# Gated MLP of an encoder block: the down-projection sums two row tiles in PSUM, convolution and gate keep their running value there, and the up products share three banks

## The chip, the core and the metric

The kernel is one program on one core of a Trainium2 chip. TensorE (PE in the profile; PEld is its weight load) multiplies into PSUM, which has eight banks of 512 float32 columns; VectorE (DVE) and ScalarE (ACT) read and write PSUM and SBUF; GpSimd (POOL) works on SBUF alone; SyncE (SP) issues the DMAs. The metric is device time in microseconds (us) of one launch. Lower is better.

## What is computed

One layer on x of 2048 tokens by 1024 channels, all float32: a mixer (attention and pooling), then the channel sub-layer, to which the change is confined:

```python
h2 = rmsnorm(x, norm2_g) * (1.0 + sc2) + sh2
u  = h2 @ w_up                                   # 1024 -> 2 * 2816
u  = u[t-1]*conv_w[0] + u[t]*conv_w[1] + u[t+1]*conv_w[2] + conv_b   # per channel
gate, val = u[..., :2816], u[..., 2816:]
out = x + g2 * ((silu(gate) * val) @ w_down)
```

## The kernel before

Every float32 matrix operand is split into a high and a low part, and a product is three matmuls (high by high, high by low, low by high) added in PSUM.

**Tiling of the MLP.** `PARTS` cuts the tokens into three parts of 640, 768 and 640 (5, 6 and 5 row tiles of 128); each part goes through 22 steps j, one for each 128 gate channels and their 128 value channels. The loop `for idx, (p, j) in enumerate(seq)` runs 66 steps. A step does four things side by side:

- `gen_up(p, j)`: the up-projection of one gate and one value tile, as seven products of a Strassen-Winograd scheme (`PROD`), 12 matmuls each (4 of k, 3 for the split), on 322 columns (386 in the middle part). Each product has a PSUM bank of its own (tag `pp`, five of them in rotation); `add` evicts product by product, one copy on ACT and seven additions on DVE, into `ug` and `uv` in SBUF. With `kmajor` (first step of the second and third part) all seven products run side by side over k.
- `gen_gate(p, j-1)`: convolution, silu, product and split of the step before: two `Identity` on ACT, four `scalar_tensor_tensor` on DVE, `Silu` on ACT, a multiplication on DVE, a copy to `gh` on ACT and a subtraction to `gl` on DVE. The running values `ac0` and `ac1` are SBUF tiles of 640 (768) columns.
- `gen_down(p, (j-2,), n)`: `down` multiplies the gate tile j-2 with the two 512-column halves of w_down, three matmuls into a `py` bank (three in rotation) for each row tile and half, and DVE adds the bank to the running sum `ys`. Without a pair: each sum takes one row tile of w_down.
- `gen_w(p, j+1)`: the seven weight operands of the next step: POOL forms the four sums, ACT copies each operand to its high part, POOL subtracts to the low part; seven buffers of each (`whi`, `wlo`). `gen_wd` does w_down: in the first part load, multiplication by the gate `g2` and subtraction on DVE, copy on ACT, and a store to DRAM; in later parts two loads.

**Order.** The generators are advanced by hand-written counts of up matmuls (`n % 11`, `n % 8`, `WS`); a planner then orders each engine's queue by data and free buffers, with the written order as priority, except instructions held by `keep_in_program_order`. On the chip each engine takes its queue in order. Between two parts `gen_ops` prepares seven moving operands for the next part, 4 k-slices each, on ACT, POOL and DVE, beside the last downs of the part; at the very end the last three row tiles are summed in `pl` banks and stored.

Of the kernel before, what the change touches and what calls it, by code (L numbers as in the profile page):

```python
# [18 lines left out]
P = 128  # L19
# [28 lines left out]
class InOrder:  # L48
    """An engine whose instructions stay in the order in which they are written."""
# [15 lines left out]
def hybrid_block(ctx: ExitStack, tc: tile.TileContext, x, c, w_ada, b_ada, norm1_g, w_in,  # L65
# [58 lines left out]
    # =============== mixer input projection ===============  # L124
    with tc.tile_pool(name="p1", bufs=1) as p1, \
            tc.tile_pool(name="ps1", bufs=1, space=PSUM) as ps1:
        # columns of w_in: q, k, v first (their space is free first), then u
# [173 lines left out]
        # scale and shift of the first norm; the first tokens' norm beside them  # L301
# [18 lines left out]
        # weights, split, in the order of use  # L320
# [19 lines left out]
        # 1/count at the clipped edges  # L340
# [108 lines left out]
        def gen_tr(tok, qhl, khl):  # L449
            """q as (hi, lo), k as (hi, hi) and (lo, one), transposed"""  # L450
# [25 lines left out]
        def windows(b, us, res):  # L476
            """column i is token t0 - 8 + i, at column 8 + i of u; the last block has 8 more"""
# [74 lines left out]
        def gen_early_max():  # L552
            """the row maxima of the first unit over the keys of the blocks that are done"""
# [75 lines left out]
    # =============== attention and output projection ===============  # L629
    ctx3 = ctx.enter_context(ExitStack())  # L630
    with tc.tile_pool(name="po", bufs=1, side="right", reuse_waits="tile") as po, \
# [8 lines left out]
        # per key tile: [v_lo 0 | v_hi 0 | ones | v_hi 1 | v_lo 1]  # L640
# [185 lines left out]
        def gen_out(c_, half, wait=0):  # L826
            """x1 = x + pool half, then x1 += attention half."""
# [17 lines left out]
        def gen_ln2(t, x1, junk, hts, bank, stat, wait):  # L845
            """normalised x1, transposed"""
# [31 lines left out]
        # the last chunk's output projection: the pool half first, in banks that the attention leaves  # L878
# [67 lines left out]
        # =============== gated conv MLP: Winograd's form of Strassen's product ===============  # L946
# [12 lines left out]
        def gen_ops(p, res):  # L959
            """the moving operands of part p, split"""  # L960
# [10 lines left out]
            for k in range(4):  # L971
# [35 lines left out]
                G.tensor_tensor(out=t2, in0=t2, in1=b21, op=ALU.subtract)  # L1007
# [7 lines left out]
        def gen_w(p, j, res):  # L1015
            """the stationary operands of one pair of column tiles, split, in the order of use"""
# [12 lines left out]
            def split(nm, src):  # L1029
                h_ = pv.tile([P, 4, P], F32R, tag="whi", name=f"wh_{nm}{p}_{j}", bufs=7)  # L1030
                l_ = pv.tile([P, 4, P], F32R, tag="wlo", name=f"wl_{nm}{p}_{j}", bufs=7)
# [7 lines left out]
            yield  # L1039
            s1, s2 = raw2(f"s1_{p}_{j}"), raw2(f"s2_{p}_{j}")  # L1040
# [3 lines left out]
            yield  # L1044
            split("a12", a12)
# [54 lines left out]
    with tc.tile_pool(name="p3", bufs=1, reuse_waits="tile") as p3, \  # L1100
# [5 lines left out]
        def gen_wd(p, j, n, tag=""):  # L1106
            """w_down times the gate, split: worked out with the first part, kept in DRAM for the others"""
# [9 lines left out]
            h_ = pool.tile(shape, F32R, tag=tag + "hi" if tag else "wdh", name=f"wdh{p}_{j}_{n}", bufs=7 if tag else 3)  # L1117
            l_ = pool.tile(shape, F32R, tag=tag + "lo" if tag else "wdl", name=f"wdl{p}_{j}_{n}", bufs=7 if tag else 3)
# [7 lines left out]
            else:  # L1126
# [7 lines left out]
        PROD = (("1", "a11", "b11"), ("6", "s2", "t2"), ("2", "a12", "b21"), ("7", "s3", "t3"),  # L1134
                ("5", "s1", "t1"), ("4", "a22", "t4"), ("3", "s4", "b22"))

        def gen_up(p, j, kmajor, res):
            o0, no, N = PARTS[p]
            w = wres.pop((p, j))
            o = ops[p]  # L1140
            ug = p3.tile([P, 772], F32, tag="ug", name=f"ug{p}_{j}", bufs=1)
            uv = p3.tile([P, 772], F32, tag="uv", name=f"uv{p}_{j}", bufs=1)
            p1s = p3.tile([P, 386], F32, tag="p1s", name=f"p1s{p}_{j}", bufs=1)[:, 0:N]
            w1 = p3.tile([P, 386], F32, tag="w1", name=f"w1{p}_{j}", bufs=1)[:, 0:N]
# [3 lines left out]
            def bank(i):  # L1148
                py = kmajor and i < 2
                return ps3_.tile([P, 512], F32, tag="py" if py else "pp", name=f"pp{PROD[i][0]}{p}_{j}",  # L1150
                                bufs=3 if py else 5)[:, 0:N]

            def prod(ps, i, k):
                (ah, al), (bh, bl) = w[PROD[i][1]], o[PROD[i][2]]
                for m, (l_, r_) in enumerate(((ah, bh), (ah, bl), (al, bh))):
                    mm = PE.matmul(ps, l_[:, k], r_[:, k, 0:N], start=k == 0 and m == 0, stop=k == 3 and m == 2)  # L1156
# [4 lines left out]
            def add(i, ps):  # L1161
                if i == 0:
                    S.copy(out=p1s, in_=ps)
                elif i == 1:
                    V.tensor_tensor(out=w1, in0=ps, in1=p1s, op=ALU.add)
                elif i == 2:
                    V.tensor_tensor(out=ug[:, 0:N], in0=ps, in1=p1s, op=ALU.add)
                elif i == 3:
                    V.tensor_tensor(out=w7, in0=ps, in1=w1, op=ALU.add)
                elif i == 4:  # L1170
                    V.tensor_tensor(out=uv[:, N:2 * N], in0=ps, in1=w7, op=ALU.add)  # L1171
                    V.tensor_tensor(out=w1, in0=ps, in1=w1, op=ALU.add)
# [101 lines left out]
        for idx, (p, j) in enumerate(seq):  # L1274
# [19 lines left out]
            for _ in gen_up(p, j, j == 0 and p > 0, res):  # L1294
# [3 lines left out]
                if n % 8 == 4:  # L1298
                    step(gate)
# [111 lines left out]
```

## Time and profile before

| | us |
|---|---|
| median of 3 runs (2737.05 to 2743.99) | 2742.21 |
| span of the profiled execution, first to last instruction | 2741.8 |
| MLP, first step to the end | 1458.5 |

The time of the profiled execution as a whole is not told apart from its span; the span lies within the three runs. Busy shares over the span: PE 95%, DVE 86%, POOL 64%, ACT 54%. The shares are means over stages with different limits: the attention fills the first half, and within the MLP the three parts differ. The page's 40 slices, the busy time by stretches, and groups of instructions within one stretch are read below.

### The profile page before, as it was taken

To read this page: it belongs to the slowest core of one execution; us is meant where nothing else is said; L and a number is where in the kernel's file an instruction comes from. 1 tells how busy PE (TensorE), PEld (TensorE's weight loads), DVE (VectorE), ACT (ScalarE), POOL (GpSimd) and SP (SyncE) were. 2 spreads that over 40 slices of the span, in tenths; PEclk is the share of its full clock that TensorE was granted. 3 is DMA by queue.
4 is the path that set the end of the run, shared out by engine and by line. 5 is a ranking of instruction groups with operands and counts; after the bars stand their busy time and mean duration, and the time that the engine had idled before them with its cause. 6 is when DMAs were issued, how large, how long until landed. Compare 5 with 4: busy or idle time off the path is not lost.

```text
span 2741.8 us, 39488 instructions
## 1 busy us (share of the span) xinstructions
PE 2594.1 (95%) x13439; PEld 2242.1 (82%) x13439; DVE 2370.5 (86%) x3526; ACT 1475.5 (54%) x2656; POOL 1767.0 (64%) x1397
## 2 busy tenths in 40 slices
PE   5899989999999999999899999899999998999999
PEld 5788867777776767767888888789999997999998
DVE  7778688989999998887999999978888888898886
ACT  5566457777778777775533443543333334533342
POOL 1222146556657666565888888697777776988883
PEclk9899989999999999999999999999999999999999
DMA  9685374331221222225444444443333224433332
GB/s 291 232 258 179 99 239 149 106 95 60 64 80 55 71 72 76 80 64 179 151 130 133 128 130 123 145 132 105 100 104 100 93 87 132 147 123 120 106 110 93
DMA packets 318164, 338.65 MB, mean 124 GB/s; under 512 B 24655, under 2 KB 226329, under 8 KB 317961
## 3 DMA queue, kind: packets, MB, share of 16 engines
q1 hardware_dynamic: 316953, 332.31, 38.4%
q0 software_dynamic: 1008, 3.81, 0.5%
q8 instruction: 106, 1.74, 0.3%
q14 instruction: 97, 0.79, 0.1%
HBM read 249.42 MB, written 86.63 MB: 123 GB/s over the span
## 4 chain that ended last, share of the span: by engine, by line
PE 36%; DVE 13%; issue 3%; ACT 1%; POOL 1%; POOLq 0%; DVEq 0%; ACTq 0%
PE pp L1156 23%; PE py L1233 13%; DVE y L1238 3%; DVE ac L1202 2%; DVE ac L1205 2%; DVE b L993 1%; DVE t L993 1%; ACT ac L1199 1%; PE pl L1354 1%; DVE wds L56 0%; DVE wdl L1123 0%; DVE ac L1212 0%; DVE ug L1176 0%; DVE uv L1171 0%; DVE uv L1174 0%
## 5 line engine op out<-in xcount | busy, mean ns | idle before, releaser
L1035 POOL TENSOR_TENSOR wl_s<-s,wh_s 128x512 fp32r<-128x512 f32 x260 | 390.3, 1502 | 187.8 <-ACT wh_s L1033 186.6
L1238 DVE TENSOR_TENSOR y<-py,y 128x512 f32<-128x512 f32 x620 | 418.5, 682 | 95.5 <-PE py L1233 94.8
L741 POOL TENSOR_TENSOR acc<-acc,ph 128x512 f32<-128x512 f32 x352 | 463.4, 1316 | 41.0 <-ACT ph L735 15.7
L1156 PE MATMUL pp<-t,wh_s 128*128 128x322 f32 (+1 forms) x1584 | 390.2, 322 | 7.0 <-DVE x L1072 3.2
L737 DVE TENSOR_TENSOR pl<-S,ph 128x512 fp32r<-128x512 f32 x512 | 348.7, 684 | 38.5 <-ACT S L736 31.5
L735 ACT ACTIVATE ph<-S 128x512 fp32r<-128x512 f32 x512 | 307.3, 600 | 131.9 <-PE S L732 116.2
L694 DVE TENSOR_REDUCE mx<-pmx 128x1 f32<-128x512 f32 x500 | 338.1, 681 | 27.0 <-PE pmx L692 25.2
L1035 POOL TENSOR_TENSOR wl_a<-wr,wh_a 128x512 fp32r<-128x512 f32 x195 | 312.9, 1605 | 22.7 <-ACT wh_a L1033 22.6
L1233 PE MATMUL py<-wdh,gh 128*128 128x512 f32 x674 | 275.7, 409 | 47.1 <-DVE y L1238 40.6
L736 ACT ACTIVATE S<-S 128x512 f32<-128x512 f32 x512 | 306.4, 598 | 0.0
L1156 PEld LDWEIGHTS pp<-t,wh_s 128*128 128x128 f32 x1584 | 282.2, 190 | 27.8 <-DVE t L993 4.1
L1033 ACT CAST wh_s<-s 128x512 fp32r<-128x512 f32 x264 | 161.9, 617 | 226.8 <-PE pp L1156 197.0
L1156 PE MATMUL pp<-b,wh_a 128*128 128x322 f32 (+1 forms) x1056 | 267.9, 323 | 1.3 <-DVE b L993 0.8
L1233 PE MATMUL py<-wdh,gl 128*128 128x512 f32 x674 | 268.8, 399 | 0.0
L1233 PE MATMUL py<-wdl,gh 128*128 128x512 f32 x674 | 268.8, 399 | 0.0
L1156 PE MATMUL pp<-t,wl_s 128*128 128x322 f32 (+1 forms) x792 | 254.3, 321 | 0.0
L724 PE MATMUL B<-pl,vt 128*128 128x512 f32 x512 | 210.5, 411 | 6.2 <-DVE pl L737 6.0
L1033 ACT CAST wh_a<-wr 128x512 fp32r<-128x512 f32 x198 | 122.3, 618 | 165.6 <-PE pp L1156 158.4
L723 PE MATMUL A<-ph,vt 128*128 128x512 f32 x512 | 204.7, 408 | 5.2 <-ACT ph L735 5.2
L692 PE MATMUL pmx<-kA,qa 128*128 128x512 f32 x500 | 203.3, 408 | 3.9 <-DMA kA<-k_scr 3.0
L739 POOL TENSOR_TENSOR acc<-ph,ph 128x512 f32<-128x512 f32 x32 | 41.3, 1290 | 256.8 <-ACT ph L735 226.9
L732 PE MATMUL S<-qb,kB 65*128 65x512 f32 x512 | 202.8, 402 | 1.1 <-ACT qb L702 0.8
(273 smaller groups left out, 6784.4 us busy)
## 6 DMA issues: line engine op xcount, KB each, us to landing
wr<-in_w_up_dram SPq DMA_DIRECT2D x132, 512.0 KB
wdh<-wd_scr SPq DMA_DIRECT2D x88, 256.0 KB
wdl<-wd_scr SPq DMA_DIRECT2D x88, 256.0 KB
stage<-in_w_ada_dram SPq DMA_DIRECT2D x36, 512.0 KB
x_scr<-x SPq DMA_DIRECT2D x48, 256.0 KB
wds<-in_w_down_dram SPq DMA_DIRECT2D x44, 256.0 KB
wd_scr<-wdh SPq DMA_DIRECT2D x44, 256.0 KB
wd_scr<-wdl SPq DMA_DIRECT2D x44, 256.0 KB
```

Source lines behind the costliest of these rows:

```text
L694: V.tensor_reduce(out=mx[:, qt, j:j + 1], in_=ps, axis=AX.X, op=ALU.max)
L723: PE.matmul(A, vt[:, kt, 192 * a:192 * a + P], ph, start=kt == 0, stop=kt == NKT - 1)
L724: PE.matmul(B, vt[:, kt, 64 + 64 * a:192 + 64 * a], pl, start=kt == 0, stop=False)
L735: S.activation(out=ph, in_=s, func=AF.Exp, scale=0.125)
L736: S.activation(out=s, in_=s, func=AF.Exp, scale=0.125)
L737: V.tensor_tensor(out=pl, in0=s, in1=ph.bitcast(F32), op=ALU.subtract)
L741: G.tensor_tensor(out=acc, in0=acc, in1=ph.bitcast(F32), op=ALU.add)
L1033: S.copy(out=hf, in_=src)
L1035: eng.tensor_tensor(out=lf, in0=src, in1=hf.bitcast(F32), op=ALU.subtract)
L1156: mm = PE.matmul(ps, l_[:, k], r_[:, k, 0:N], start=k == 0 and m == 0, stop=k == 3 and m == 2)
L1233: PE.matmul(ps, l_[:, ts_], r_, start=i == 0, stop=i == 3 * len(js) - 1)
L1238: V.tensor_tensor(out=ys[t][:, ns], in0=ps, in1=ys[t][:, ns], op=ALU.add)
```

## The change

- **Down-projection**: from step 3 on every second step runs downs, for the pair (j-3, j-2): six matmuls into one `py` bank, then one addition by DVE. Even steps have none. The last two steps of a part have none; the pair (L-3, L-2) goes into the change of parts (L is 21). The four w_down tiles of a pair have four buffers instead of three, and their work is spread as before, two a step.
- **Gate**: one PSUM tile `ac` of two banks holds the running value, first of the gate half, then of the value half; `Silu` writes an SBUF tile `ag`. `ug`, `uv`, `ag`, `gh`, `gl` share eight SBUF tiles (`utile`); before there was one `ug` and one `uv`.
- **Up products**: banks `px`, `pz`, `pw`, one of each. Products 1, 6, 5 are added up in `px` and 7, 4 in `pw` by the matmuls themselves; ACT copies the partial sums out between them (four copies instead of one), DVE adds four times instead of seven. The operand order becomes a11, a12, s2, s3, s1, a22, s4, and t4 has its sign turned. `whi` and `wlo` have six buffers instead of seven, that is fewer by one weight operand ahead.
- Counts of the interleaving change (`n % 7` for the gate, `76` for the downs, `WS`); the last halves go in another order. Removed comments do nothing.

```diff
             def split(nm, src):
-                h_ = pv.tile([P, 4, P], F32R, tag="whi", name=f"wh_{nm}{p}_{j}", bufs=7)
+                h_ = pv.tile([P, 4, P], F32R, tag="whi", name=f"wh_{nm}{p}_{j}", bufs=6)
...
+        def utile(nm, dtype=F32):
+            return p3.tile([P, 772], dtype, tag="u", name=nm, bufs=8)
...
-            ug = p3.tile([P, 772], F32, tag="ug", name=f"ug{p}_{j}", bufs=1)
-            uv = p3.tile([P, 772], F32, tag="uv", name=f"uv{p}_{j}", bufs=1)
+            ug, uv = (utile(f"{nm}{p}_{j}") for nm in ("ug", "uv"))
...
-                for i in range(7):
-                    ps = bank(i)
-                    for k in range(4):
-                        yield from prod(ps, i, k)
-                    add(i, ps)
+            X, Y, W = bank("px"), bank("pz"), bank("pw")
+            yield from run(X, "1")
+            S.copy(out=p1s, in_=X)
+            yield from run(Y, "2")
+            add(c11, Y, p1s)
+            yield from run(X, "6", False)
+            S.copy(out=u2s, in_=X)
+            yield from run(W, "7")
+            S.copy(out=w7, in_=W)
+            yield from run(X, "5", False)
+            add(c22, X, w7)
+            u3s = p3.tile([P, 386], F32, tag="p1s", name=f"u3s{p}_{j}", bufs=1)[:, 0:N]
+            S.copy(out=u3s, in_=X)
+            yield from run(W, "4", False)
+            add(c21, W, u2s)
+            Y = bank("pz")
+            yield from run(Y, "3")
+            add(c12, Y, u3s)
+        def ac_tile(nm):
+            return ps3_.tile([P, 1024], F32, tag="ac", name=nm, bufs=1)
...
-                t_ = p3.tile([P, 768], F32, tag=f"ac{gv}", name=f"ac{gv}{p}_{j}", bufs=1)[:, 0:no]
+                t_ = ac_tile(f"ac{gv}{p}_{j}")[:, 0:no]
...
                 if gv == 0:
-                    S.activation(out=t_, in_=t_, func=AF.Silu)
+                    ag = utile(f"ag{p}_{j}")[:, 0:no]
+                    S.activation(out=ag, in_=t_, func=AF.Silu)
...
-            V.tensor_tensor(out=ag, in0=ag, in1=av, op=ALU.mult)
+            V.tensor_tensor(out=t_, in0=t_, in1=ag, op=ALU.mult)
...
-            dn = chain2(gen_down(p, (j - 2,), 0, add), gen_down(p, (j - 2,), 1, add)) if 2 <= j < L else iter(())
+            dn = iter(())
+            if j % 2 and 3 <= j < L:
+                add = [residual(p, i) for i in (j - 3, j - 2) if p > 0 and i < 2 * nt]
+                dn = chain2(gen_down(p, (j - 3, j - 2), 0, add), gen_down(p, (j - 3, j - 2), 1, add))
+            wdg = chain2(*(ahead if p == 0 else wd_of(p, j)))
...
-                if (n - 4) * 2 * nt >= done * 78:
+                if (n - 6) * 2 * nt >= done * 76:
                     step(dn)
...
                 for n in range(2):
-                    dn = gen_down(p, (L - 2,), n)
+                    dn = gen_down(p, (L - 3, L - 2), n)
                     while step(dn):
-                        step(gate, G1)
-                        step(opg, O1 if n else O0)
+                        step(gate, 2)
+                        step(opg, n)
```

## Rows read from the trace of the kernel before

**Rows 1.** Busy time by stretches of the MLP; the first line names the columns.

```profile
core 0: us, PE busy (x) PEld busy (x) DVE busy (x) ACT busy (x) POOL busy (x), PEclk, DMA share, GB/s
1283.30:1367.80 84.50, 76.27 (x442) 71.56 (x443) 70.58 (x78) 43.56 (x75) 71.55 (x49) 0.92 0.54 170
1367.80:1478.40 110.60, 99.59 (x568) 89.73 (x567) 109.03 (x139) 42.66 (x71) 95.99 (x58) 1.00 0.44 136
1478.40:1731.10 252.70, 238.93 (x1373) 217.31 (x1373) 247.99 (x326) 102.54 (x170) 206.64 (x133) 1.00 0.41 125
1731.10:1842.00 110.90, 96.38 (x455) 83.48 (x454) 88.90 (x111) 58.87 (x101) 86.78 (x61) 0.92 0.44 142
1842.00:2257.30 415.30, 415.30 (x2157) 387.62 (x2156) 345.96 (x460) 152.13 (x218) 296.25 (x201) 1.00 0.31 98
2257.30:2360.00 102.70, 92.48 (x487) 82.06 (x486) 81.89 (x108) 53.15 (x95) 77.27 (x63) 0.95 0.44 143
2360.00:2706.30 346.30, 346.30 (x2042) 323.09 (x2041) 309.75 (x423) 139.04 (x216) 298.13 (x200) 1.00 0.35 111
```

**Rows 2.** Timeline of ACT in the first part: start, us, what.

```profile
1583.70 0.42 ACT L1163 COPY p1s<-pp 128x322 f32<-128x322 f32 x1
...
1604.75 0.42 ACT L1163 COPY p1s<-pp 128x322 f32<-128x322 f32 x1
```

**Rows 3.** Chain of work that ended last: start, us, what, how many.

```profile
1859.88 2.12 PE pp L1156 x12
1883.03 2.12 PE pp L1156 x12
...
2374.06 1.92 PE pp L1156 x13
2393.42 1.92 PE pp L1156 x13
```

**Rows 4.** The same chain inside one step of the third part.

```profile
2391.55 1.18 PE pp L1156 x8
2392.72 0.70 PE py L1233 x3
```

**Rows 5.** Groups in twelve steps of part one: busy us, mean ns | idle before.

```profile
L1238 DVE TENSOR_TENSOR y<-py,y 128x512 f32<-128x512 f32 x120 | 80.4, 678 | 0.0
...
L56 DVE TENSOR_TENSOR wds<-wds,gate 128x512 f32<-128x512 f32 x24 | 29.4, 1226 | 0.0
...
L1123 DVE TENSOR_TENSOR wdl<-wds,wdh 128x512 fp32r<-128x512 f32 x24 | 23.4, 976 | 0.0
...
L1212 DVE TENSOR_TENSOR ac<-ac,ac 128x640 f32<-128x640 f32 x12 | 21.8, 1815 | 0.0
...
L1205 DVE SCALAR_TENSOR_TENSOR ac<-uv,cols,ac 128x640 f32<-128x640 f32 x13 | 19.6, 1510 | 0.0
...
L1199 ACT ACTIVATE ac<-uv,cols 128x640 f32<-128x640 f32 x12 | 11.1, 924 | 24.1 <-DVE uv L1174 24.1
L1205 DVE SCALAR_TENSOR_TENSOR ac<-ug,cols,ac 128x640 f32<-128x640 f32 x12 | 10.4, 870 | 0.0
...
L1165 DVE TENSOR_TENSOR w<-pp,p1s 128x322 f32<-128x322 f32 x12 | 5.8, 482 | 0.0
```

**Rows 6.** Waits in the same stretch: us in total, times, longest.

```profile
ACT ac L1208 <- DVE ac L1205: 54.5, 12, 4.5
...
PE py L1233 <- DVE y L1238: 13.8, 24, 0.9
```

**Rows 7.** Timeline of all engines in a step of the third part.

```profile
2436.36 0.42 ACT L1163 COPY p1s<-pp 128x322 f32<-128x322 f32 x1
2436.47 0.46 PE L1156 MATMUL pp<-t,wh_s 128*128 128x322 f32 x2
...
2438.93 0.46 PE L1156 MATMUL pp<-b,wh_a 128*128 128x322 f32 x2
...
2442.35 0.48 DVE L1165 TENSOR_TENSOR w<-pp,p1s 128x322 f32<-128x322 f32 x1
```

More of the change, by code (lines that the diff above doesn't have):

```diff
@@ L1159, in prod, with run @@
                     yield
[L1161 to L1172, printed above, removed]
-                elif i == 5:
-                    V.tensor_tensor(out=uv[:, 0:N], in0=w7, in1=ps, op=ALU.subtract)
-                else:
-                    V.tensor_tensor(out=ug[:, N:2 * N], in0=ps, in1=w1, op=ALU.add)
+            def run(ps, nm, first=True):
+                for k in range(4):
+                    yield from prod(ps, nm, k, first)
@@ L1178, in gen_up, with add @@
+            def add(out, ps, b):
+                V.tensor_tensor(out=out, in0=ps, in1=b, op=ALU.add)
             if kmajor:
-                banks = [bank(i) for i in range(7)]
+                ac = ac_tile(f"acu{p}_{j}")
+                banks = {"1": bank("px"), "2": bank("pz"), "6": bank("py"), "7": bank("pw"),
+                         "5": ac[:, 0:N], "4": ac[:, 512:512 + N]}
                 for k in range(4):
-                    for i in range(7):
-                        yield from prod(banks[i], i, k)
@@ L1183, in gen_up @@
-                for i in range(7):
-                    add(i, banks[i])
-            else:
-                for i in range(7):
-                    ps = bank(i)
-                    for k in range(4):
-                        yield from prod(ps, i, k)
-                    add(i, ps)
+                    for nm, ps in banks.items():
+                        yield from prod(ps, nm, k)
+                S.copy(out=p1s, in_=banks["1"])
+                add(u2s, banks["6"], p1s)
+                add(c11, banks["2"], p1s)
@@ new lines, in gen_up @@
+                X = bank("px")
+                yield from run(X, "3")
+                add(w7, banks["7"], u2s)
+                add(c22, banks["5"], w7)
+                add(u2s, banks["5"], u2s)
+                add(c21, banks["4"], w7)
+                add(c12, X, u2s)
+                return
+            X, Y, W = bank("px"), bank("pz"), bank("pw")
[4 more added lines that the diff above has]
+            yield from run(X, "6", False)
@@ L1273, in hybrid_block, with wd_of @@
         held = iter(())
+        ahead = []
+        def wd_of(p, j):
+            a = j - 2 - j % 2
+            return [gen_wd(p, a + i, j % 2) for i in range(2)] if 2 <= j < NF else []
         for idx, (p, j) in enumerate(seq):
@@ L1316, in hybrid_block @@
             if p == 0 and j < L:
-                ahead = [gen_wd(p, j, n) for n in range(1 if j + 1 == L else 2)]
+                ahead = wd_of(p, j + 1)
                 for g_ in ahead:
@@ L1340, in hybrid_block @@
             else:
-                drain(gate)
-                halves = [(t, n) for t in range(nt) for n in range(2)]
+                halves = [(t, n) for n in range(2) for t in range(nt)]
+                tags = ("py", "py", "py", "px", "pz", "pw", "py", "py", "py", "px")
                 ps_of = {}
@@ L1360, in part @@
                     store(p, t, n)
+                drain(gate)
                 for i in range(OPEN):
[L1363 removed]
+                    part(i, (L - 3, L - 2, L - 1))
                 for i in range(OPEN):
```

93 lines of the change are left out of this document (42 added, 51 removed).

## The prediction

> **What bounds the kernel now.** The change touches the MLP alone, the last 1458.5 us, so I read busy time by stretches there first [rows 1]. The stretches are cut where the first product of a step is copied out, so they hold whole steps. The reader is to see two kinds of stretch. In the steady second and third part PE is busy for all of 415.30 and 346.30 us at a granted clock of 1.00. In twelve steady steps of the first part (1478.4 to 1731.1) DVE is busy 247.99 of 252.70 us and PE 238.93. Around them lie three poor stretches, the start and the two changes of parts, where the granted clock is 0.92, 0.92 and 0.95, that is partly the lower of its two levels.
>
> Next come step times. The first part's steps are 21.05 us apart [rows 2], the second's 23.15 and the third's 19.36 [rows 3]. First and third part have the same matmuls (84 up, 30 down), so 19.36 is what PE needs, and in the first part 1.69 us a step is lost to DVE. The chain gives PE's prices: 1.18 us for 8 up matmuls of 322 columns, 0.148 each; 0.70 for 3 down matmuls, 0.23 each [rows 4]; 2.12 for 12 of 386 columns, 0.177 each [rows 3]. 84 x 0.148 + 30 x 0.23 is 19.3, and 84 x 0.177 + 36 x 0.23 is 23.15: PE needs no more than its matmuls there. What PE waits for in the first part is the eviction of a `py` bank: 13.8 us in 24 waits [rows 6].
>
> So I count PE time lost, stretch by stretch (length less matmuls at those prices; the transposes of the last norm count as lost):
> - start, first four steps: 84.5 less 4 x 12.4 less 2 x 6.95 = 21
> - 17 steps of part one: 363.3 less 17 x 19.36 = 34
> - change to part two: 110.9 less 86.4 (72 matmuls of the last step 10.6, three downs 20.9, three steps and a product of part two 46.6, one down 8.3) = 24.5
> - part two and three: nothing
> - change to part three: 102.7 less 83.6 (12.7, 24.9, 39, 7) = 19
> - the end, from 2706.3: 35.5 less 31.5 = 4
>
> Together 102 us. The change moves matmuls but neither adds nor removes one, so it can win only from these.
>
> **The change, part by part.** *Down sums in pairs.* DVE's evictions fall from ten a step to five on average in part one: 5 x 0.60 (0.678 each, less 0.08 by which neighbours overlap) = 3.0 us off DVE a step [rows 5]. PE's downs all move to odd steps: 12.4 us for an even step (14.9 in part two), 26.2 for an odd one (31.4). PE's sum stays.
>
> *Up products in three banks.* DVE loses three additions of 0.48 (0.40 net): 1.2 us a step [rows 5]. ACT gains three copies of 0.42 [rows 2]: 1.3 us.
>
> *Gate in PSUM.* DVE's six gate operations on 640 columns take 0.87 to 1.82 us now [rows 5]. With the running value in PSUM at most one input is in SBUF. No operation writes PSUM from DVE in these rows, so I bound it: below by the slope of the PSUM readers (0.482 at 322 columns, 0.678 at 512: 0.81 at 640), above by the 1.51 of the slow form [rows 5]. I take 0.81, because the PSUM readers keep one duration beside a POOL that is busy 82% of the time, while operations with two SBUF inputs range from 0.87 to 1.82 for the same columns. The Trainium skill has the mechanism (SBUF — State Buffer, Who interferes with whom): two SBUF inputs contend with GpSimd, one does not; no run here shows it for an output in PSUM. The skill also speaks against the edit (VectorE: DVE Perf Modes, Rules for kernel authors): copy a matmul result to SBUF first if many operations follow. Going by that rule the six operations would be cheapest left in SBUF, 6 x 0.79 net = 4.7 us at the undisturbed 0.87, where I count 4.4; the rows give the copy nothing to win.
>
> DVE in an average step of part one: five evictions 3.0, four additions 1.6, six gate operations of 0.73 net 4.4, w_down 4.1 (two of 1.226 and two of 0.976, less overlap) = 13.1 us in place of 20.7 (247.99 over 12), against PE's 19.36. An even step holds all but the evictions, 10.1 of 12.4 us. So PE becomes the bound of part one, and 34 us come free, less new stalls.
>
> *New waits.* Each bank is now one of a kind. PE queues the next product behind a copy: product 5 waits until ACT has copied product 6 out of `px`, product 4 until `w7` is copied, 6 until `p1s` is; between lies one product, 12 x 0.148 = 1.77 us in an even step, 3.7 in an odd one. A copy takes 0.42, about 0.2 goes for the two signals (twice the 0.11 of [rows 7], below), and the weight cast of 512 columns that comes free at the same product end 0.67 (an estimate by columns from the copy): 1.3, so it fits unless ACT is in a longer operation or waits at its queue's head. ACT would be busy 8.5 + 1.3 = 9.8 of 12.4 us in an even step of part one, 7.7 + 1.3 = 9.0 in part three [rows 1]. For it: ACT took product 1 promptly, the next product following within 0.11 us [rows 7]. Against it: ACT stands 4.5 us a step before `Silu`, for DVE [rows 6], and what is queued behind stands with it. DVE shows how late in-order service can be: product 6 was over by 2438.93 and was read at 2442.35 [rows 7]. Bounds: nothing, or 1.5 us in each of 33 even steps. I take 1 us an even step in part one (10 us), 0.3 in part two (3) and 0.4 in part three (4).
>
> *Gate deadline.* The gate of an even tile must be ready 6 matmuls into the odd step, 12.4 + 0.9 us after it could start. Its chain is now serial in one tile: four links on ACT of at most 0.92 [rows 5], six on DVE of 0.81 and ten signals of 0.1 are 9.5 us. It fits with 3.8 us; that is the cover, and what it loses to queues is inside the stall figure.
>
> *Weights.* POOL works 206.64/12 = 17.2 us a step in part one, 16.6 in part three [rows 1]; an even step lasts 12.4. Five operands are ready ahead with six buffers, so POOL may fall 4.8 behind and catch up in the odd step. Where three steps without downs follow each other (start of a part) it may not: at the start 3 x 4.8 = 14 us remain of the 21.
>
> *Changes of parts.* One down of the old part moves here, 6.95 or 8.3 us of PE work that needs none of the next operands. The preparation is bound by DVE, ACT and POOL, not PE, so most of the moved work fills idle time: 24.5 becomes 16, 19 becomes 12, after 1 us each for the seventh product, which must wait until `px` is copied. Bounds: no gain, or 9 and 8 left.
>
> *The rest* (last halves, `t4`'s sign, spreading of w_down) has the same work in the same place: nothing. The end keeps its 4.
>
> Sum of losses after: start 14, part one 10, change 16, part two 3, change 12, part three 4, end 4 = 63, against 102 before. That is 39 us off. The profiled span of 2741.8 lies 0.4 under the median of 2742.21, so I take it off either: 2742 - 39 = 2703 us.
>
> **Rivals.**
> - *All covers hold.* No stalls (17), starts of parts as good as the bound (11): 2703 - 28 = 2675. For it: parts two and three show no idle PE although DVE evicts up to 3 us late. Against: five rotating banks took that up.
> - *The hand-offs give it back.* ACT's copies stand behind `Silu` or a cast waiting for POOL; one copy a step that is late by 0.8 us costs 62 x 0.8 = 50 us, less the 17 counted: 2703 + 33 = 2736. It decides from the point at which ACT's order puts one copy a step behind a wait.
> - *Slower: even steps run at the pace of the weights.* If each operand is tied to its step (a cast waiting for POOL's sum stands before the copy that PE needs), an even step lasts POOL's 16.6 to 17.2 us instead of 12.4 or 14.9, and the odd one gives nothing back: 10 x 4.8 + 10 x 4.2 + 11 x 1.6 = 108 on 2675, 2783. It decides once POOL is more than two operands (about 4.8 us) late; the buffers lost by one operand speak for it, the 4 us of lead I count speak against.
> - *PSUM does not relieve the gate.* At today's durations an even step of part one has 1.6 + 7.8 (20.7 less ten evictions 6.0, seven additions 2.8 and w_down) + 4.1 = 13.5 us of DVE, 1.1 over PE: 9 x 1.1 = 10, 2713.
>
> **How the numbers follow.** Chances: forecast 0.42, all covers hold 0.25, hand-offs give it back 0.17, slower 0.12, no relief 0.04. The likeliest is 2703. The range 2672 to 2745 leaves out the slower rival and the tails. 0.3% is 8 us, about what a measurement of this kernel can tell from no change. Faster (under 2734): 0.42 + 0.25 + 0.04 and a third of the hand-offs' 0.17, 0.76; same 0.10; slower 0.14.
>
> **What would show it.** Right: in part one two steps take 38.7 us together, DVE's share there falls from 98% to about 68%, gate operations on DVE take 0.8 us with little spread, and the first change of parts is shorter. Wrong: PE waiting in up products for ACT copies by more than 1 us a step, weight casts ending PE's waits in even steps, or gate operations above 1 us. If parts two and three get longer by more than 15 us together, the hand-offs were under-priced.

## The result and the profile after

The changed kernel takes 2694.33 us (median of 4 runs, 2691.69 to 2695.23) against 2742.16 before: a ratio of 0.9828 [0.9814, 0.9842], 47.8 us less. The forecast was 2703, with 2672 to 2745. The profiled execution spans 2692.6 us, before 2741.8.

First the page, line 1, then busy time by stretches; columns as in [rows 1]. Each stretch again begins where product 1 of a step is copied out (steps 0, 4 and 21 of part one, 3 and 21 of part two, 3 and 21 of part three).

```profile
PE 2577.8 (96%) x13439; PEld 2232.5 (83%) x13439; DVE 1926.2 (72%) x3014; ACT 1544.4 (57%) x2848; POOL 1615.7 (60%) x1397
```

```profile
1282.90:1359.20 76.30, 70.92 (x428) 66.81 (x427) 35.37 (x49) 44.84 (x83) 62.72 (x48) 0.96 0.48 153
1359.20:1687.80 328.60, 326.44 (x1914) 302.59 (x1914) 238.85 (x323) 165.71 (x291) 266.37 (x185) 1.00 0.44 143
1687.80:1790.90 103.10, 93.67 (x456) 81.42 (x455) 69.18 (x104) 57.78 (x100) 73.55 (x61) 0.97 0.52 165
1790.90:2207.40 416.50, 416.50 (x2157) 387.94 (x2156) 218.14 (x287) 175.84 (x283) 257.40 (x201) 1.00 0.32 99
2207.40:2301.30 93.90, 89.39 (x488) 79.81 (x487) 62.22 (x98) 52.04 (x96) 68.36 (x66) 1.00 0.49 154
2301.30:2649.80 348.50, 348.50 (x2048) 324.71 (x2047) 187.27 (x269) 161.87 (x280) 255.40 (x199) 1.00 0.36 111
```

In part one PE is now busy 326.44 of 328.60 us and DVE 238.85, that is 73%. Parts two and three are all PE, as before. DVE has fewer instructions in each part and ACT more, as the copies moved. The granted clock rose to 0.96, 0.97 and 1.00 in the three poor stretches.

The prediction's budget, filled in by the same prices. Downs sit on odd steps now, so the cuts hold a little more or less of PE's work than before, and each stretch has its own floor (part one: 9 steps of 12.41 and 8 of 26.31). us:

| stretch | length before | lost before | length after | matmuls after | lost after | predicted lost |
|---|---|---|---|---|---|---|
| start | 84.5 | 21 | 76.3 | 63.5 | 12.8 | 14 |
| part one | 363.3 | 34 | 328.6 | 322.2 | 6.4 | 10 |
| change to part two | 110.9 | 24.5 | 103.1 | 85.0 | 18.1 | 16 |
| part two | 415.3 | 0 | 416.5 | 416.7 | 0 | 3 |
| change to part three | 102.7 | 19 | 93.9 | 84.9 | 9.0 | 12 |
| part three | 346.3 | 0 | 348.5 | 348.5 | 0 | 4 |
| end | 35.5 | 4 | 42.8 | 38.5 | 4.3 | 4 |
| sum | | 102 | | | 51 | 63 |

(The start before, counted from the first copy of product 1 as after, is 82.6, which makes 19 of its 21 lost.) 102 less 51 is 51; the spans differ by 49.2, as the cuts of the start differ and the prices are rounded.

The instruments of part one: groups of DVE from 1479.2 to 1687.8, then a pair of steps in ACT's timeline, then all waits of PE in the whole of part one.

```profile
L1253 DVE TENSOR_TENSOR y<-py,y 128x512 f32<-128x512 f32 x50 | 34.4, 688 | 32.2 <-PE py L1248 31.7
L1123 DVE TENSOR_TENSOR wdl<-wds,wdh 128x512 fp32r<-128x512 f32 x23 | 23.6, 1028 | 0.0
...
L1221 DVE SCALAR_TENSOR_TENSOR ac<-uv,cols,ac 128x640 f32<-128x640 f32 x11 | 9.8, 889 | 6.3 <-ACT ac L1218 6.3
...
L1224 DVE SCALAR_TENSOR_TENSOR ac<-ug,cols,ac 128x640 f32<-128x640 f32 x11 | 9.7, 879 | 0.0
L1231 DVE TENSOR_TENSOR ac<-ac,ag 128x640 f32<-128x640 f32 x11 | 9.0, 820 | 0.0
L1236 DVE TENSOR_TENSOR gl<-ac,gh 128x640 fp32r<-128x640 f32 x11 | 9.0, 820 | 2.2 <-ACT gh L1234 2.2
```

```profile
1571.09 0.42 ACT L1192 COPY p1s<-px 128x322 f32<-128x322 f32 x1
1596.37 0.42 ACT L1192 COPY p1s<-px 128x322 f32<-128x322 f32 x1
...
1610.16 0.42 ACT L1192 COPY p1s<-px 128x322 f32<-128x322 f32 x1
```

```profile
PE px L1159 <- ACT u2s L1196: 1.4, 2, 1.2
PE pz L1159 <- DVE ug L1170: 0.8, 1, 0.8
```

The six gate operations, 0.87 to 1.82 us before [rows 5], take 0.82 to 0.89. The eviction of a `py` bank keeps its 0.69 us and comes half as often. A pair of steps takes 39.07 us (38.7 of matmuls), where two steps took 42.1 [rows 2]. PE's waits of 13.8 us for `py` in twelve steps [rows 6] are gone, and the new hand-offs, one to ACT and one to DVE, cost 2.2 us in all of part one.

### The profile page after: what moved, and what is told of

The parts are those of the page before. It is cut to its first block, busy times and chain, and to the rows that moved or that the text cites. A ratio compares the mean times of both kernels' runs of the same rounds, so it can differ in the third digit from the quotient of the medians.

```text
span 2692.6 us, 38997 instructions
## 1 busy us (share of the span) xinstructions
PE 2577.8 (96%) x13439; PEld 2232.5 (83%) x13439; DVE 1926.2 (72%) x3014; ACT 1544.4 (57%) x2848; POOL 1615.7 (60%) x1397
## 4 chain that ended last, share of the span: by engine, by line
PE 47%; DVE 2%; POOL 1%; ACT 1%; issue 1%; DMA 0%; DVEq 0%; SPq 0%; POOLq 0%; ACTq 0%
PE py L1248 16%; PE px L1159 13%; PE pw L1159 9%; PE pz L1159 8%; PE pl L1377 1%; DVE b L993 0%; POOL wl_s L1035 0%; ACT hb L977 0%; POOL t L1000 0%; DVE y L1253 0%; DMA wr<-in_w_up_dram 0%; POOL t L1007 0%; POOL wl_a L1035 0%; ACT ac L1218 0%; DVE t L993 0%
## 5 line engine op out<-in xcount | busy, mean ns | idle before, releaser
L1035 POOL TENSOR_TENSOR wl_s<-s,wh_s 128x512 fp32r<-128x512 f32 x260 | 349.6, 1346 | 204.7 <-ACT wh_s L1033 202.1
L1253 DVE TENSOR_TENSOR y<-py,y 128x512 f32<-128x512 f32 x300 | 205.8, 688 | 222.4 <-PE py L1248 220.7
L1035 POOL TENSOR_TENSOR wl_a<-wr,wh_a 128x512 fp32r<-128x512 f32 x195 | 266.7, 1374 | 104.7 <-ACT wh_a L1033 104.3
L1248 PE MATMUL py<-wdh,gh 128*128 128x512 f32 x664 | 261.7, 395 | 1.9 <-DVE y L1253 1.7
L1248 PE MATMUL py<-wdh,gl 128*128 128x512 f32 x664 | 262.1, 395 | 0.0
L1248 PE MATMUL py<-wdl,gh 128*128 128x512 f32 x664 | 261.8, 395 | 0.0
L1159 PE MATMUL px<-t,wh_s 128*128 128x322 f32 (+1 forms) x1024 | 247.9, 322 | 5.3 <-ACT p1s L1192 3.6
L731 PE MATMUL S<-qa,kA 128*128 128x512 f32 x512 | 202.4, 398 | 0.0
L1159 PEld LDWEIGHTS px<-t,wh_s 128*128 128x128 f32 x1024 | 178.3, 189 | 12.3 <-ACT p1s L1192 4.4
L1159 PE MATMUL px<-t,wl_s 128*128 128x322 f32 (+1 forms) x512 | 164.2, 321 | 0.0
```

The costliest lines, as they stand in the source:

```text
L1159: mm = PE.matmul(ps, l_[:, k], r_[:, k, 0:N], start=first and k == 0 and m == 0, stop=k == 3 and m == 2, skip_group_check=not first)
L1248: PE.matmul(ps, l_[:, ts_], r_, start=i == 0, stop=i == 3 * len(js) - 1)
L1253: V.tensor_tensor(out=ys[t][:, ns], in0=ps, in1=ys[t][:, ns], op=ALU.add)
```

## The experiments

Theory, from the prediction's steps: part one is freed because DVE falls below PE, the hand-offs to ACT and POOL's lead hold, and the moved downs shorten the changes of parts. Rivals: the gain hangs on one of the three edits alone; a late copy or POOL's pace decides; the changes of parts have another cause. Each expectation says which theory stands for what.

Stage lengths of all kernels, from the same copies. The time of the first copy belongs to the unchanged attention part, and its spread of some 11 us is in every total beside the edit; so the verdicts rest on stages. Each ratio is against the kernel before as timed beside that run (medians of 2740.47 to 2742.67 us).

| kernel | median us | ratio [95%] | first copy | start | part one | change 1 | part two | change 2 | part three | end |
|---|---|---|---|---|---|---|---|---|---|---|
| before | 2742.16 | 1 | 1285.1 | 82.6 | 363.3 | 110.9 | 415.3 | 102.7 | 346.3 | 35.4 |
| after | 2694.33 | 0.9828 [0.9814, 0.9842] | 1282.9 | 76.3 | 328.6 | 103.2 | 416.5 | 93.9 | 348.6 | 42.8 |
| e1_unpaired | 2704.81 | 0.9874 [0.9859, 0.9889] | 1284.2 | 76.2 | 330.0 | 106.1 | 416.5 | 99.2 | 348.6 | 42.8 |
| e2_gate_only | 2690.78 | 0.9817 [0.9803, 0.9832] | 1283.6 | 77.3 | 329.3 | 101.0 | 415.6 | 98.1 | 347.4 | 36.0 |
| e3_up_only | 2769.12 | 1.0102 [1.0085, 1.0119] | 1284.1 | 85.9 | 370.9 | 114.9 | 416.3 | 109.2 | 348.1 | 36.0 |
| e4_pool_no_read | 2682.01 | 0.9787 [0.9772, 0.9801] | 1282.2 | 69.9 | 328.4 | 101.4 | 415.6 | 99.1 | 347.4 | 35.4 |
| e5_no_g2 | 2698.24 | 0.9842 [0.9823, 0.9861] | 1282.4 | 77.7 | 331.4 | 105.5 | 415.3 | 101.7 | 346.3 | 35.4 |
| e6_copy4 | 2704.43 | 0.9863 [0.9842, 0.9884] | 1288.7 | 77.5 | 328.7 | 103.6 | 418.3 | 94.8 | 351.6 | 43.0 |
| e7_pool_more | 2721.06 | 0.9921 [0.9899, 0.9944] | 1288.5 | 84.1 | 327.8 | 112.4 | 416.1 | 102.3 | 347.9 | 42.8 |
| e8_downs_back | 2715.39 | 0.9903 [0.9878, 0.9927] | 1278.4 | 76.0 | 329.0 | 113.4 | 417.4 | 103.6 | 347.6 | 42.9 |
| e9_prep_early | 2691.62 | 0.9812 [0.9798, 0.9825] | 1284.6 | 76.3 | 328.7 | 99.7 | 416.5 | 93.6 | 348.6 | 42.8 |
| e10_gate_prep | 2690.64 | 0.981 [0.9796, 0.9823] | 1285.6 | 76.9 | 328.0 | 103.0 | 415.6 | 97.2 | 347.4 | 36.0 |
| e11_gate_up | 2698.2 | 0.9833 [0.982, 0.9847] | 1289.9 | 77.8 | 328.9 | 103.8 | 416.3 | 100.9 | 347.9 | 36.0 |
| e12_low_on_dve | 2696.87 | 0.9845 [0.9831, 0.9858] | 1281.7 | 75.0 | 328.6 | 105.2 | 416.5 | 96.4 | 348.4 | 42.9 |

**The pairs undone in the changed kernel.** In `gen_down`, each tile of a pair gets its own bank and eviction:

```diff
-                down(p, js, n, t)
+                for j_ in ((j,) for j in js) if js[-1] < L else (js,):
+                    down(p, j_, n, t)
```

> The changed kernel with the pairing of the down sums undone: odd steps still run the downs of two tiles, but each tile has a sum of its own, three matmuls and one DVE addition, ten (twelve) additions more in an odd step. Theory A (budget): in part one a step lasts as long as the longer of DVE's work and PE's 19.36 us; DVE rises by 3.0 us a step to about 16.5, still under 19.36, so the time stays within 5 us of the changed kernel (2690 to 2700), part one at 39 to 39.5 us for two steps. Theory B (the pairing itself brought the gain, because PE had waited for evictions of py banks): about 25 us slower, near 2720.

Part one grows by 1.4 us only, although DVE evicts ten banks more in a pair of steps. Most of the rest of the 10.5 is in the changes of parts (2.9 and 5.3), which theory A had not counted. So, beside the other two edits, the pairs are not what freed part one; they help in the changes.

**The gate alone, on the kernel before.** One PSUM tile holds the running value; the banks come from `pp`, five to three.

```diff
-                t_ = p3.tile([P, 768], F32, tag=f"ac{gv}", name=f"ac{gv}{p}_{j}", bufs=1)[:, 0:no]
+                t_ = ac_tile(f"ac{gv}{p}_{j}")[:, 0:no]
...
-                    S.activation(out=t_, in_=t_, func=AF.Silu)
+                    sg = p3.tile([P, 768], F32, tag="sg", name=f"sg{p}_{j}", bufs=1)[:, 0:no]
+                    S.activation(out=sg, in_=t_, func=AF.Silu)
```

> The kernel before with the gate's running value in PSUM alone: one two-bank tile for both halves, three banks for the seven products in place of five, silu into an SBUF tile. Downs and up sums as before. Theory A (budget): DVE falls by some 3 us from 20.7 to about 17.7 us a step in part one, under PE's 19.36, so part one goes from 21.06 to about 19.5 us a step and the time to about 2715. Theory B (pairing): ten evictions a step as before, no change, 2735 to 2745. If three banks are too few for products that DVE evicts, slower than 2742.

This one edit gives the whole gain. Groups of DVE in twelve steps of part one, and the stretch from 1500 to 1700:

```profile
L1123 DVE TENSOR_TENSOR wdl<-wds,wdh 128x512 fp32r<-128x512 f32 x24 | 33.5, 1395 | 1.0 <-ACT wdh L1122 1.0
L56 DVE TENSOR_TENSOR wds<-wds,gate 128x512 f32<-128x512 f32 x24 | 16.3, 680 | 0.0
L1212 DVE SCALAR_TENSOR_TENSOR ac<-ug,cols,ac 128x640 f32<-128x640 f32 x13 | 11.6, 889 | 0.4
```

```profile
1500.00:1700.00 200.00, 200.00 (x1190) 187.49 (x1189) 182.70 (x280) 94.59 (x147) 160.89 (x116) 1.00 0.44 137
```

DVE is still busy 182.70 of 200 us, but PE all of it: in part one DVE had only to fall under PE, and how far under is worth nothing. The total came 24 us under the 2715 of theory A, as the start and the changes got shorter too (5.3, 9.9 and 4.6 us). With the stages added up, from the first copy on, the kernel before takes 1456.5 us, the gate alone 1404.7 and all three edits 1409.9: beside the gate, the other two edits together win nothing.

**The up products alone, on the kernel before.** `gen_up` and the operand order as in the changed kernel, gate and downs as before.

```diff
-                for i in range(7):
-                    ps = bank(i)
...
+            X, Y, W = bank("px"), bank("pz"), bank("pw")
+            yield from run(X, "1")
+            S.copy(out=p1s, in_=X)
```

> The kernel before with the up products in three banks alone (four copies on ACT, four additions on DVE, the new operand order; seven weight buffers kept). Theory A (budget): DVE falls by 1.2 us to 19.5 us a step, about PE's 19.36: part one at 19.6 to 19.9 us a step, time near 2720. Theory B (pairing): no change. Theory C (the hand-offs of the shared banks cost PE time, hidden in the changed kernel): parts two and three get longer by more than 10 us and the time is at or over 2742.

28 us slower than before by the ratio, with fewer DVE instructions; part one is 7.6 us longer, the start 3.3, the changes 4.0 and 6.5. Theory A is refuted. Of theory C the total came, its sign did not: parts two and three are only 1.0 and 1.8 us longer. DVE's groups in twelve steps (1485 to 1741), two waits, ACT's timeline in one step with PE's matmul that waits for it, and the stretch from 1501 to 1715:

```profile
L1239 DVE TENSOR_TENSOR gl<-ac,gh 128x640 fp32r<-128x640 f32 x12 | 19.2, 1604 | 0.0
...
L1223 DVE SCALAR_TENSOR_TENSOR ac<-ug,cols,ac 128x640 f32<-128x640 f32 x12 | 14.9, 1238 | 0.0
```

```profile
ACT ac L1226 <- DVE ac L1223: 56.5, 12, 4.8
...
PE px L1157 <- ACT u2s L1194: 20.0, 12, 1.8
```

```profile
1552.50 0.74 ACT L1226 ACTIVATE ac<-ac 128x640 f32<-128x640 f32 x1 [4.80 <-DVE ac L1223]
...
1555.83 0.72 ACT L1237 CAST gh<-ac 128x640 fp32r<-128x640 f32 x1 [1.51 <-DVE ac L1230]
1556.46 0.61 ACT L1033 CAST wh_s<-s 128x512 fp32r<-128x512 f32 x1
1556.98 0.42 ACT L1194 COPY u2s<-px 128x322 f32<-128x322 f32 x1
...
1557.45 0.56 PE L1157 MATMUL px<-t,wh_s 128*128 128x322 f32 x2 [1.77 <-ACT u2s L1194]
```

```profile
1501.00:1715.00 214.00, 196.96 (x1134) 181.17 (x1134) 208.34 (x239) 96.71 (x169) 168.11 (x110) 0.99 0.39 121
```

This is the prediction's rival of the hand-offs, in its own words: the copy `u2s` stands on ACT behind `Silu`, which waits 4.80 us for DVE, and behind `gh`, which waits 1.51 more; PE waits 1.77 us, once in every step. DVE is busy 208.34 of 214 us all the same: `gl` takes 1604 ns here against 1313 before, the operation ahead of `Silu` 1238 against 870 [rows 5]. What three evictions less freed went into longer operations. The traces show why they are longer. One `gl` before, then one here, each with the POOL instruction that began ahead of it:

```profile
1510.54 1.75 POOL L1035 TENSOR_TENSOR wl_s<-s,wh_s 128x512 fp32r<-128x512 f32 x1
1511.65 1.32 DVE L1221 TENSOR_TENSOR gl<-ac,gh 128x640 fp32r<-128x640 f32 x1
```

```profile
1514.34 1.29 POOL L1035 TENSOR_TENSOR wl_s<-s,wh_s 128x512 fp32r<-128x512 f32 x1 [2.04 <-ACT wh_s L1033]
1514.71 1.60 DVE L1239 TENSOR_TENSOR gl<-ac,gh 128x640 fp32r<-128x640 f32 x1
```

Both end 0.68 us after POOL's instruction does; here `gl` begins earlier in it and so lasts longer. The operation ahead of `Silu` ran beside no POOL instruction in all twelve steps before (0.87 us), and here behind one in ten of twelve (1.31). So the edit, which also changes the order of POOL's operands, moved DVE's operations against POOL's.

**POOL without its reads, on the kernel before.**

```diff
-                eng.tensor_tensor(out=lf, in0=src, in1=hf.bitcast(F32), op=ALU.subtract)
+                eng.memset(lf.bitcast(F32), 0.0)
```

> The kernel before, in which POOL writes zeros into the low parts of the w_up operands in place of the subtraction (so the low parts are left out); POOL then reads SBUF only for the four sums a step. Theory A with contention: DVE's operations with two SBUF inputs fall towards 0.87 (640 columns) and 0.68 (512), DVE from 20.7 to about 17 us a step, part one to 19.4 to 19.7 us a step, time about 2714. Rival: the long durations are DVE's own and stay; part one stays at 21.06 and the time at 2742.

Nothing on DVE was edited, and part one goes to PE's floor. The total is 32 us under the 2714 of theory A: the start is 12.7 us shorter, the changes 9.5 and 3.6. The same groups:

```profile
L1212 DVE TENSOR_TENSOR ac<-ac,ac 128x640 f32<-128x640 f32 x13 | 22.2, 1711 | 0.0
L1123 DVE TENSOR_TENSOR wdl<-wds,wdh 128x512 fp32r<-128x512 f32 x24 | 16.2, 676 | 0.0
L56 DVE TENSOR_TENSOR wds<-wds,gate 128x512 f32<-128x512 f32 x23 | 15.6, 678 | 0.0
...
L1205 DVE SCALAR_TENSOR_TENSOR ac<-uv,cols,ac 128x640 f32<-128x640 f32 x12 | 10.5, 877 | 0.0
```

With two inputs in SBUF, `wds` falls from 1226 to 678 ns, `wdl` from 976 to 676, `L1205 uv` from 1510 to 877. The product `ac<-ac,ac` stays slow. The 1226 ns of before are a mean of two lengths, 1.77 us in twelve cases and 0.68 in the other twelve. One of each kind before, then `wds` and the product in this run:

```profile
1500.58 1.87 POOL L1035 TENSOR_TENSOR wl_a<-wr,wh_a 128x512 fp32r<-128x512 f32 x1
1501.22 1.77 DVE L56 TENSOR_TENSOR wds<-wds,gate 128x512 f32<-128x512 f32 x1
...
1504.91 0.68 DVE L56 TENSOR_TENSOR wds<-wds,gate 128x512 f32<-128x512 f32 x1
```

```profile
1509.80 0.53 POOL L1035 MEMSET wl_s<- 128x512 f32 x1 [2.62 <-PE pp L1156]
1509.86 0.68 DVE L56 TENSOR_TENSOR wds<-wds,gate 128x512 f32<-128x512 f32 x1
...
1510.70 1.30 POOL L1055 TENSOR_TENSOR s<-wr,s 128x512 f32<-128x512 f32 x1 [0.37 <-ACT wh_s L1033]
1510.86 1.81 DVE L1212 TENSOR_TENSOR ac<-ac,ac 128x640 f32<-128x640 f32 x1
...
1696.57 0.82 DVE L1212 TENSOR_TENSOR ac<-ac,ac 128x640 f32<-128x640 f32 x1
```

The long `wds` began behind a subtraction of POOL, the short one beside nothing; behind a fill it is short too. The product began behind one of POOL's four sums in twelve of thirteen cases (1.53 to 1.82 us), and took 0.82 the one time that POOL was idle. So what held DVE over PE's pace in part one was POOL's reads. The Trainium skill (SBUF — State Buffer, Who interferes with whom) says that a DVE operation with two SBUF inputs contends with a POOL instruction that reads SBUF, not with one that only writes it. These traces agree: 1.77 us behind the subtraction, 0.68 behind the fill. The run also takes the start to 69.9, the lowest of all.

**One DVE operation less, on the kernel before.**

```diff
-                MU.tensor_tensor(out=src, in0=src, in1=gate2[:, ns], op=ALU.mult)
```

> The kernel before without the multiplication of w_down by the gate g2 in part one (left out): two DVE operations of 1.23 us a step less, nothing else touched. Theory A (budget): DVE falls by 2.3 to 18.4 us a step, PE becomes the bound of part one at 19.4 to 19.6 us a step, time about 2717. Theory B (only fewer evictions help): 2735 to 2745.

Two operations of 1.226 us on average less a step [rows 5], and part one falls from 363.3 to 331.4, against 328.6 after the change: some 2.5 us off DVE is nearly enough. The total came 19 us under the 2717 of theory A, as the start and the first change got shorter too (4.9 and 5.4 us).

**Longer copies in the changed kernel.**

```diff
-            S.copy(out=u2s, in_=X)
+            for _ in range(4):
+                S.copy(out=u2s, in_=X)
```

and the same for `w7`.

> The changed kernel with each of ACT's two tight copies (u2s after product 6, w7 after product 7) made four times in a row, so that the bank comes free about 1.0 us later and ACT has 2 us more a step. Slack theory: 0.2 + 1.4 us still fits in the 1.77 us of an even step's product (2.1 in part two), so 5 to 20 us slower at most, from queueing. Rival (the hand-offs stand at their edge): 1.0 us for each of two hand-offs in 31 even steps, some 60 us slower, 2755.

Each of these hand-offs is 3 x 0.42 = 1.3 us later, and part one stays at 328.7; parts two and three give 1.8 and 3.0. The hand-off has slack of about that size where ACT is not held at its head. The 10 us of the median lie in the range of the slack theory; of the 13.6 by which the two profiled executions differ, 5.8 lie ahead of the first copy.

**POOL slower in the changed kernel.**

```diff
-            E.tensor_tensor(out=s3, in0=a11, in1=a21, op=ALU.subtract)
+            for _ in range(3):
+                E.tensor_tensor(out=s3, in0=a11, in1=a21, op=ALU.subtract)
```

> The changed kernel with POOL forming s3 three times over: two more operations of 1.3 us, about 2.7 us a step. Lead theory: POOL then works about 18 us a step in part one and 17 in the others, over an even step's 12.4 but under the mean of 19.36 or 23.15, and five operands lie ahead, so no more than 8 us slower, at the starts of parts. Rival (even steps tied to the weights): 2.7 us in 31 even steps, 80 us slower, 2775.

Part one as a stretch (1372.6 to 1700.4), with two groups of DVE in it:

```profile
1372.60:1700.40 327.80, 326.12 (x1909) 301.81 (x1908) 241.25 (x323) 164.40 (x291) 305.14 (x217) 1.00 0.44 143
```

```profile
L1124 DVE TENSOR_TENSOR wdl<-wds,wdh 128x512 fp32r<-128x512 f32 x22 | 26.1, 1189 | 0.0
...
L1222 DVE SCALAR_TENSOR_TENSOR ac<-uv,cols,ac 128x640 f32<-128x640 f32 x11 | 9.8, 888 | 6.9 <-ACT ac L1219 6.9
```

POOL is busy 305.14 of 327.80 us and part one is no longer. The lead of five operands carries the even steps at a POOL of 17.9 us a step; the rival "even steps at the pace of the weights" falls for part one. It holds where no odd step with downs pays back: start 7.8 us longer, the changes 9.2 and 8.4. The expected 8 us in all were short; the kernel is 27 us slower. The rows show a second thing: `wdl`, with both inputs in SBUF, grew from 1028 to 1189 ns, the gate operation into PSUM kept its 888.

**The moved downs put back, in the changed kernel.**

```diff
-            if j % 2 and 3 <= j < L:
+            if j % 2 and 3 <= j < (L if p + 1 == len(PARTS) else NF):
...
-                    dn = gen_down(p, (L - 3, L - 2), n)
+                    dn = iter(range(nt))
```

> The changed kernel with the downs of tiles 18 and 19 back in the last step of a part (parts one and two) instead of in the change of parts. Theory (the moved downs fill idle PE time while the next operands are prepared): steps get longer and the changes shorter by less, 8 to 16 us slower in all. Rival (the changes of parts got shorter only by DVE's relief): no difference, within 3 us.

The changes are 10.2 and 9.7 us longer, together more than the 8 to 16 us expected in all. PE's longest wait in each (1683 to 1797, then 2202 to 2310):

```profile
PE py L1248 <- ACT wdh L1122: 10.9, 2, 10.6
...
PE py L1248 <- ACT gh L1234: 7.6, 1, 7.6
```

In the change to part three PE stands 7.6 us before the last gate product, with no down left to fill the time: as expected. In the change to part two it stands 10.6 us before a tile of w_down, whose work kept the changed kernel's spread over the steps and came too late for the earlier downs. That wait is of the experiment's own making, so this run tells nothing about the first change. The kernels without pairs tell: there the first change takes 101.0 (gate alone) and 103.8 (gate and up) against 103.2, no difference; the second takes 98.1 and 100.9 against 93.9.

**Preparing the next part earlier.** In the changed kernel `step(opg, 1)` in both halves, with the gate alone `O0` 1 instead of 0:

```diff
-                        step(opg, n)
+                        step(opg, 1)
```

> The changed kernel with the preparation of the next part's operands begun one loop of downs earlier (one step of it also beside the first five or six down sums of a change of parts). Theory (the changes of parts are bound by the preparation, 18 and 9 us of PE time lost there): both get shorter by 3 to 6 us, 2682 to 2690. Rival (its place in the written order does not matter, since the queues run ahead anyway): within 3 us of the changed kernel.

> The kernel before with the gate's value in PSUM (the earlier experiment, 2690.8) and the preparation begun one loop earlier. Same theory: changes of parts of 101.0 and 98.1 us get shorter by 2 to 4 us each, 2683 to 2687. Rival: within 3 us of 2691.

In the changed kernel the first change falls by 3.5 us, the second by 0.3; with the gate alone the first is 2.0 longer and the second 0.9 shorter. Medians move by 2.7 and 0.1 us, inside the intervals. The rival holds in both totals; the theory had one of four changes right.

**Gate and up products together, downs unpaired in every step, on the kernel before** (the edits of e2 and e3 in one).

> The kernel before with the gate in PSUM and the up products in three banks, downs unpaired and in every step. The up products alone made the kernel 28 us slower: in part one PE waited 1.7 us a step for ACT's copy u2s, which stood behind silu waiting for DVE. Theory (that wait comes from the slow gate on DVE, so with the gate relieved it goes): part one at 19.4 to 19.7 us a step, time 2690 to 2700. Rival (the shared banks cost by themselves wherever downs run in every step): part one at 20 us a step or more, 2710 to 2720.

Part one, 1367.6 to 1696.5:

```profile
1367.60:1696.50 328.90, 328.90 (x1938) 306.86 (x1937) 292.57 (x411) 167.90 (x290) 256.37 (x191) 1.00 0.45 142
```

The same `gen_up` that lost 28 us alone leaves no wait of PE here. With the gate in PSUM, ACT is no longer held before `Silu`, and the copy comes in time: the theory's range held. So e3's loss in part one was the slow gate, reached through ACT's order.

**Two low parts moved from POOL to DVE**, on e9, to use DVE's idle time:

```diff
-        VS = ((), (), ())
+        VS = (("s1", "a22"),) * 3
```

> The changed kernel with the early preparation and two of the seven low parts of each step's weights (s1, a22) subtracted by DVE instead of POOL: POOL has some 3 us a step less, DVE 1.2 more. Theory (with DVE relieved, POOL's weights bound the steps without downs at the starts of parts; three times s3 had made the three starts 8 to 9 us longer each for 2.7 us a step): start and changes of parts 2 to 4 us shorter each, 2680 to 2686. Rival (the starts wait for other things, or DVE's additions come later for the extra work): no shorter, 2688 to 2700.

Part one keeps its 328.6, as it is PE's; start 1.3 us shorter, the changes 5.5 and 2.8 longer than in e9. Not faster, as the rival had it.

Not tried: the changed kernel with its gate back in SBUF, and the pairs alone on the kernel before. That the pairs alone would free part one follows from the sum, and e5 speaks for it, but e3 shows that such a sum can fail; it is not shown. No kernel beats the changed one by more than the intervals, but for e4, which leaves work out.

## Why the prediction was right, and where its terms were off

**The bound and the threshold: right.** DVE held part one, PE holds it now. The stretch came out at 328.6 with pairs of steps of 39.07 us (38.7 forecast); what gave it was DVE falling under 19.36 us a step. The gate alone does that (e2), and neither the pairs (e1) nor the up products were needed for it. That three edits gave about the forecast gain says nothing for the other two.

**Gate in PSUM: right in kind, short in size.** 0.81 was taken for all six; the two with tile inputs alone measure 0.82, the four `SCALAR_TENSOR_TENSOR` 0.88 to 0.89. They do not move with POOL's load (888 ns at 266.37 and at 305.14 us of POOL), which the prediction could only argue by way of operations reading PSUM. In the changed kernel the product takes 0.82 us behind a reading POOL instruction, as here, and just as much beside none:

```profile
1563.24 1.75 POOL L1035 TENSOR_TENSOR wl_s<-s,wh_s 128x512 fp32r<-128x512 f32 x1
1563.77 0.82 DVE L1231 TENSOR_TENSOR ac<-ac,ag 128x640 f32<-128x640 f32 x1
```

The Trainium skill (VectorE: DVE Perf Modes, Rules for kernel authors) offers two ways for elementwise work on a matmul result: accept the 1x rate of a PSUM source, or copy it to SBUF first if many operations follow. The prediction named the second alone, as speaking against the edit. The running value is no matmul result, and keeping it in PSUM wins here: gate alone is 50 us faster by the ratio. Beside a POOL that reads, operations with two SBUF inputs took up to 1.82 us and the PSUM ones 0.82 to 0.89.

**The DVE sum: right on the side, wrong as arithmetic.** The prediction added three savings (3.0, 1.2, 3.4) and got 13.1 us a step; 238.85 over 17 is 14.0. The four gate operations at 0.07 more are 0.3 of the excess, four additions of the residual that the sum left out 0.4; most of the rest is that neighbours overlap by 0.05 us each and not by 0.08. But the sum does not hold edit by edit: the up products should have freed 1.2 us a step, and alone they made the kernel 28 us slower. DVE's durations before are contended ones, and what they cost depends on when POOL's instructions begin, so removed work can come back as longer neighbours (`gl` 1313 to 1604 ns). The prediction put the three into one sum; by that sum the gate alone was already enough (20.7 less 3.4 is 17.3), and so were the pairs (17.7), and it did not say so.

**Hand-off stalls: priced too high.** 10, 3 and 4 us were put down by choice between two bounds. Part one lost 6.4 (of which PE waited 2.2; in the rest it was busy a little beyond the prices), the steady parts two and three nothing: 10.6 of the 12 us by which the sum was off. e6 shows why: in part one the hand-off bears 1.3 us more at no cost. The rival behind it is real, but e3 shows its point: ACT's head must wait on DVE. With the gate in PSUM that wait shrank with the gate.

**Weights: right.** The start kept 12.8 us (14 predicted). By the first copies its three steps without downs last 18.0, 17.8 and 15.6 us where PE needs 12.4, and 20.9, 20.3 and 18.8 with 2.7 us more of POOL a step (e7): POOL's pace sets them. It is not alone, as 3 us less of POOL won 1.3 us there (e12). The steady even steps did not slow.

**Changes of parts: near in sum by luck, wrong in cause for the first.** 16 and 12 were predicted, 18.1 and 9.0 measured; the two misses make up for each other. The 8.5 us off the first were put down to the moved downs; with the gate alone and no downs moved it is 101.0 us, as short, and in e4, with no DVE operation edited, 101.4. There the evictions had been late: PE waited 8.2 us for DVE before `py` in the old change (the first line below), and after the change it has no such wait, only 6.9 us for ACT's preparation of the next operands (the second).

```profile
PE py L1233 <- DVE y L1238: 8.2, 5, 5.2
...
PE pw L1159 <- ACT t L992: 6.9, 4, 3.3
```

In the second change pairs and moved downs count, but only together: 93.9 us with both, 99.2 with the moved downs alone (e1), 103.6 with the pairs alone (e8), 97.2 to 100.9 with neither (e2, e10, e11).

**The rest.** The end lost its 4 again, and the last halves brought no surprise. The granted clock is in no term of the sum, but in what it calls lost. In the two changes together the matmuls of the MLP are the same by the prices (170.0 and 169.9 us), and PE is busy 188.9 us before [rows 1] and 183.1 after, at clocks of 0.92 and 0.95 before, 0.97 and 1.00 after. So 5.8 of the 16.6 us that the changes got shorter are busy time and not waits. That goes with the higher clock; no run shows it apart from the rest.

**Rivals.** "All covers hold" (2675) lies lower than measured, because starts and changes keep their floor and part one lost 6.4; parts two and three did hold. "PSUM does not relieve the gate" is refuted by the groups above. "The hand-offs give it back" and "slower" did not come in the steady steps, as e6 and e7 show.

## What to carry to other kernels

Read an engine's durations by form before adding up what an edit saves: where the same operation shows several lengths for one size, look what ran beside each length, because a mean over them (1226 ns here) may be the length of none. If the excess belongs to a neighbour, the edit that takes an operand out of that contention (a running value in PSUM instead of SBUF) can be worth more than taking instructions away. It only has to bring the engine under the next bound; beyond that, further relief is worth nothing in that stage and may only add hand-offs. Before PE is made to wait for a copy on an in-order engine, look what else stands ahead of that copy and whom it waits for.

## What the runs showed of the hardware

- A DVE operation with two inputs in SBUF has more than one length here. On 512 columns it took 0.68 us beside no POOL instruction or behind a fill, and 1.77 where a subtraction of POOL had begun 0.64 us ahead of it; on 640 columns 0.82 and 1.81. Both ended about 0.55 us (512) and 0.68 us (640) after POOL's instruction, so the length tells how much of that was left, and the profile counts the waiting as busy time. Where DVE began first (e2), the same operation took 0.68 beside a POOL that reads.
- With one of the two tile inputs in PSUM, the 640-column forms kept 0.82 (two tile inputs) and 0.88 to 0.89 us (two and a column of factors) at any POOL load seen.
- Relief doesn't add up under contention: three PSUM evictions less left DVE as busy as before (97% of 214 us), by operations that grew by up to 0.37 us each on average, because they then began at other points of POOL's instructions.
- A 0.42 us copy behind two waiting instructions on ACT held PE for 1.7 us in each of twelve steps (20.0 in all), in a kernel with three DVE evictions a step less whose part one was 7.6 us longer.
